# Linear attention with both heads of a pair in one 128-row product, and the low parts of keys written in place

## The chip, the cores and the metric

The kernel runs on one core of a Trainium2 chip. The metric is the time of the whole program on the device, in microseconds. TensorE is called PE here, its weight loads PEld, VectorE DVE, ScalarE ACT, GpSimd POOL and SyncE SP; SP issues nearly all DMAs.

## The reference

Two transformer blocks over 512 tokens of 1024 features. The first mixes gated linear attention (4 heads of 64), sliding-window attention (8 query heads, 2 key heads of 64), a pooling branch and gates, then a feed-forward layer. The second has forgetting attention (16 heads of 64), a feed-forward layer, latent attention and a feed-forward layer. What the change touches:

```python
# linear attention, per head; b is the running sum of log gates in a chunk
attn = einsum('bhid,bhjd,bhijd->bhij', q, k, exp(b_i - b_j))     # j <= i
o    = einsum('bhij,bhjv->bhiv', attn, v) + einsum('bhid,bhdv->bhiv', q * exp(b), S)
# window attention and forgetting attention, per head
s = einsum('qd,kd->qk', q, k) * 64 ** -0.5      # + mask, or + gate bias; then softmax, then @ v
```

## The kernel before

Activations lie with features on partitions and tokens along the free axis. A projection is made for 128 outputs at a time: eight 128-row blocks of inputs, each block with three f32r products of 512 columns (high by high, high by low, low by high; `mm3`, line 347). Weights stream through SP into `raw`, ACT makes the high part, DVE the low part (`lo`, line 277).

Each attention is a Python generator. Every matmul that is recorded adds to a counter (`clock`, line 338), and `tick` resumes a generator once the counter passes its due time. The table `LAG` holds the due times. So the order of PE's instructions is fixed by these numbers; a scheduler orders those of the other engines. At most four generators are active. All PSUM banks (8) are shared by everything, and so are 39 SBUF slots of 4 KB a partition.

**Linear attention** (`gla`, line 678) builds for each head the 512 masked weights in `A`: one diagonal product and seven levels with distance s = 64, 32, ... 1. For each level `mixed` multiplies the keys on one side and the queries on the other by decay factors (DVE d, ACT exponential, POOL and DVE `mix`), and `masked` makes four products of 128 by 128 for each of four heads. A head has 64 features, and so these products have 64 rows; they are f32. A masked copy on DVE (line 703) brings each bank into `A`. Later come the states `S` between blocks of 128 tokens, and the outputs `o`, where full-row products by `A` and 64-row products by `S` take turns. The result is wanted only when gate a begins, long after the pooling projections `pu`, the gate projections `gr` and the gates c and b. The PE instructions of the mixer follow in the order gv, sv, sk, sq, pu, gr, poolw, gate c, gate b, gate a.

**Scores** of the window attention (`swa`) and of the forgetting attention (`fox`) have queries `Q` with the high part in 64 rows and the low part in the other 64, so that one product by `K` (high part of the key in both halves) makes two terms; a second by `L` (low part) adds the rest. `stack_k` (line 432) makes KH on ACT and KL on DVE and copies each half four times by DMA. The forgetting attention does so for eight pairs of heads, the window attention once.

Of the kernel before, what the change touches and what calls it, by code (L numbers as in the profile page):

```python
# [24 lines left out]
LEVELS = (64, 32, 16, 8, 4, 2, 1)  # L25
# [130 lines left out]
def tfk_kept(e):  # L156
# [12 lines left out]
    "last": 2.8, "last_rsqrt": 3.7,  # L169
    "decay": 8.0, "level": 1.85, "mask": 1.22, "state": 6.5, "kt": 1.44, "U": 1.95, "osq": 4.41, "gnorm": 6.82, "gbc": 0.8,  # L170
    "fox_gap": 4.38, "mla_gap": 4.48, "swa_gap": 3.75, "swa": 4.0, "swa_soft": 14.0, "swa_pt": 8.0, "fox": 6.04, "fox_soft": 22.08, "fox_last": 0.8, "fox_pt": 4.44,
# [24 lines left out]
class Net:  # L196
    def __init__(self, ctx, tc, xin, wall, par, cst, msk, nar, out, dbg=None):
        self.tc, self.nc = tc, tc.nc
        nc = self.nc
# [5 lines left out]
        self.psum = ctx.enter_context(tc.tile_pool(name="psum", bufs=8, space=bass.MemoryType.PSUM))  # L205
        self.nslot, self.nt2 = 39, 9
        self.x = [self.slot([P, 2, T], F32, "x") for _ in range(4)]
# [5 lines left out]
        self.ones = self.cpool.tile([P, P], F32, name="ones")  # L213
        nc.gpsimd.memset(self.ones, 1.0)
        self.ident = self.c("ident", 128)
        self.unit_at = 0
# [215 lines left out]
    def stack_k(self, k):  # L432

        nc = self.nc
        out = K, L = [self.slot([P, 2, T], F32R, n) for n in ("K", "L")]
        parts = [self.t2(dt=F32R, name=n) for n in ("KH", "KL")]
        nc.scalar.copy(out=parts[0], in_=k)
        nc.vector.tensor_tensor(out=parts[1], in0=k, in1=parts[0].bitcast(F32), op=ALU.subtract)
        for a, b in zip(out, parts):
            for j in range(2):  # L440
                for r in range(2):
                    nc.sync.dma_start(out=a[64 * r:64 * r + 64, j].bitcast(F32), in_=b[64 * j:64 * j + 64].bitcast(F32))
        return K, L

    def mm_stacked(self, out, Q, K, L, j, qs, ks):

        self.mm(out, Q[:, j, qs], K[:, j, ks], True, False)
        self.mm(out, Q[:, j, qs], L[:, j, ks], False, True)

# [126 lines left out]
    def mixer(self, nxt):  # L576
        nc, v = self.nc, self.nc.vector
# [4 lines left out]
        glow = self.narrow("glow")  # L582
# [4 lines left out]
        pl = self.proj_narrow(glow, self.xs)  # L587
# [3 lines left out]
        rsb, rst = self.rs.get()  # L591
        glow = self.t2([16, T], F32, "glow")
        v.tensor_tensor(out=glow, in0=self.add_narrow(pl, 32, 16), in1=rsb[0:16], op=ALU.mult)
        b = self.slot([P, 2, T], F32, "b")
# [6 lines left out]
        for f in range(2):  # L601
            ps = first[f]
# [75 lines left out]
    def gla(self, glow, b, kT, qT, vtok, fut):  # L678
        nc, v = self.nc, self.nc.vector
        reset = self.c("reset", 512)  # L680
        for f in range(2):
            pz = self.ps("z")
            self.mm(pz, self.c("gup", 256)[0:16, f * P:(f + 1) * P], glow, True, True)
            la = self.t2(name="la")
            self.log_sigmoid(pz, self.p("b_gate", f), (P, T), la)
            v.tensor_tensor_scan(out=b[:, f], data0=reset, data1=la, initial=0.0, op0=ALU.mult, op1=ALU.add)
            yield LAG["decay"]
        A = [self.slot([P, 2, T], F32, "A") for _ in range(2)]
        Ah = [A[h // 2][:, h % 2] for h in range(4)]
        for a in A:  # L690
            nc.gpsimd.memset(a, 0.0)
        while not self.qk_ready:
            yield 1.0
        yield 1.0

        def masked(li, mixq, mixk):
            for h in range(4):
                f, r = h // 2, slice(64 * (h % 2), 64 * (h % 2) + 64)
                ps = self.ps("lev")
                for m in range(4):  # L700
                    c = slice(m * P, (m + 1) * P)
                    self.mm(ps[:, c], mixk[r, f, c], mixq[r, f, c], True, True)
                v.copy_predicated(
                    out=Ah[h].rearrange("p (m i) -> p m i", m=4), mask=self.msk[:, li].unsqueeze(1).to_broadcast([P, 4, P]),
                    data=ps.rearrange("p (m i) -> p m i", m=4))
                yield LAG["mask"]

        def mixed(s):
# [5 lines left out]
            d = self.slot([P, 2, T], F32, "d")  # L714
            mix = self.slot([P, 2, T], F32, "mix")
            bv, dv, mv = view(b), view(d), view(mix)
# [4 lines left out]
            nc.gpsimd.tensor_tensor(out=mv[:, :, 0:s], in0=dv[:, :, 0:s], in1=view(kT)[:, :, 0:s], op=ALU.mult)  # L721
            v.tensor_tensor(out=mv[:, :, s:], in0=dv[:, :, s:], in1=view(qT)[:, :, s:], op=ALU.mult)
            return mix

        nxt = mixed(LEVELS[0])
        yield from masked(len(LEVELS), qT, kT)
        for li, s in enumerate(LEVELS):
            mix = nxt
            if li + 1 < len(LEVELS):
                nxt = mixed(LEVELS[li + 1])  # L730
            yield LAG["level"]
            yield from masked(li, mix, mix)

# [35 lines left out]
        for h in range(4):  # L769
            f, r = h // 2, slice(64 * (h % 2), 64 * (h % 2) + 64)  # L770
# [32 lines left out]
    def swa(self, t, g, q, k, V, of, fut):  # L803
# [13 lines left out]
        for n in range(4):  # L817
            lo, out = where(n)
            keys = slice(max(n - 1, 0) * P, (n + 1) * P)
            self.mm_stacked(out, q, *k, g, slice(n * P, (n + 1) * P), keys)  # L820
        for n in range(4):
# [216 lines left out]
    def fox(self, nxt):  # L1038
# [40 lines left out]
        def head(h, q, k, bias, of, fut):  # L1079
# [6 lines left out]
            m0 = self.tiny([P, 4], F32, "m0")  # L1086
            for n in range(4):
                w = (n + 1) * P
                self.mm_stacked(sc[n], q, *k, j, slice(n * P, w), slice(0, w))
            for n in range(4):  # L1090
# [297 lines left out]
```

## Time and profile before

| | |
|---|---|
| Time before, median of 3 runs | 2256.32 us (2255.63 to 2258.09) |
| The profiled execution | 2253.59 us |
| Its span | 2251.7 us |
| Mean granted clock of PE | 0.991 |
| PE busy | 2196.6 us (98%) |
| DVE busy | 1415.0 us (63%) |
| ACT busy | 1020.5 us (45%) |

The mixer's linear and window attention lie between about 62 and 207 us, the forgetting attention between about 850 and 1110. PE's busy time is modelled from its records and also covers time in which its pipe only empties; so a stretch is read by the starts of its instructions. A matmul in f32 leaves two records, one in f32r leaves one.

### The profile page before, as it was taken

To read this page: it belongs to the slowest core of one execution; us is meant where nothing else is said; L and a number is where in the kernel's file an instruction comes from. 1 tells how busy PE (TensorE), PEld (TensorE's weight loads), DVE (VectorE), ACT (ScalarE), POOL (GpSimd) and SP (SyncE) were. 2 spreads that over 40 slices of the span, in tenths; PEclk is the share of its full clock that TensorE was granted. 3 is DMA by queue.
4 is the path that set the end of the run, shared out by engine and by line. 5 is a ranking of instruction groups with operands and counts; after the bars stand their busy time and mean duration, and the time that the engine had idled before them with its cause. 6 is when DMAs were issued, how large, how long until landed. Compare 5 with 4: busy or idle time off the path is not lost.

```text
span 2251.7 us, 27823 instructions
## 1 busy us (share of the span) xinstructions
PE 2196.6 (98%) x10664; PEld 1837.5 (82%) x10664; DVE 1415.0 (63%) x2349; ACT 1020.5 (45%) x1672; POOL 279.2 (12%) x231
## 2 busy tenths in 40 slices
PE   8999999999999998988999999999999999999998
PEld 6778888898888897867888888887888888888887
DVE  7798445578776247657667775357656557777624
ACT  4354333444444235556544443235756665444322
POOL 4122000040000003445200000102100101000000
PEclk9999999999999999999999999999999999999998
DMA  4201333332333343634233333332122213333232
GB/s 161 76 29 57 96 101 94 113 94 69 101 94 98 99 131 116 167 105 112 76 94 100 97 94 101 96 108 75 57 66 66 75 57 94 94 100 97 94 101 96
DMA packets 64838, 211.04 MB, mean 94 GB/s; under 512 B 7728, under 2 KB 10160, under 8 KB 64704
## 3 DMA queue, kind: packets, MB, share of 16 engines
q1 hardware_dynamic: 64272, 208.46, 30.9%
q8 instruction: 84, 1.38, 0.3%
q10 hardware_dynamic: 432, 0.79, 0.1%
q14 instruction: 50, 0.41, 0.1%
HBM read 197.65 MB, written 2.13 MB: 89 GB/s over the span
## 4 chain that ended last, share of the span: by engine, by line
PE 85%; DVE 8%; ACT 3%; DMA 2%; issue 2%; SPq 1%; POOL 0%; DVEq 0%; ACTq 0%; POOLq 0%
PE up L339 31%; PE down L339 15%; PE mout L339 4%; PE uq L339 3%; PE sc L339 3%; PE gate_a L339 2%; PE gate_b L339 2%; PE gate_c L339 2%; PE fout L339 2%; PE wout L339 2%; DVE lo L277 2%; PE lev L339 1%; DVE xs L420 1%; PE mpo L339 1%; PE dq L339 1%
## 5 line engine op out<-in xcount | busy, mean ns | idle before, releaser
L277 DVE TENSOR_TENSOR lo<-raw,hi 128x1024 fp32r<-128x1024 f32 (+1 forms) x348 | 438.4, 1260 | 327.2 <-ACT hi L276 322.8
L339 PE MATMUL up<-xs,hi 128*128 128x512 f32 x2016 | 621.7, 390 | 0.0
L276 ACT CAST hi<-raw 128x1024 fp32r<-128x1024 f32 (+1 forms) x348 | 365.3, 1050 | 563.6 <-PE down L339 171.8
L339 PEld LDWEIGHTS up<-xs,hi 128*128 128x128 f32 x2016 | 378.2, 188 | 79.5 <-issue 1.0
L339 PE MATMUL up<-xs,lo 128*128 128x512 f32 x1008 | 392.2, 389 | 0.0
L339 PE MATMUL down<-hl,hi 128*128 128x512 f32 (+1 forms) x1188 | 332.9, 366 | 0.0
L339 PEld LDWEIGHTS down<-hl,hi 128*128 128x128 f32 x1188 | 214.8, 189 | 36.4
L339 PEld LDWEIGHTS up<-xs,lo 128*128 128x128 f32 x1008 | 189.2, 188 | 39.1
L339 PE MATMUL down<-hl,lo 128*128 128x512 f32 (+1 forms) x594 | 217.1, 365 | 0.0
L503 POOL TENSOR_TENSOR acc<-acc,sq 128x256 f32<-128x256 f32 (+1 forms) x48 | 56.1, 1169 | 765.2 <-ACT sq L500 763.5
L980 DVE TENSOR_TENSOR u<-up,rsb 128x512 f32<-128x512 f32 x132 | 90.2, 686 | 80.9 <-PE up L339 76.7
L982 ACT ACTIVATE c<-u,par 128x512 f32<-128x512 f32 x132 | 107.0, 814 | 60.0 <-DVE u L980 59.8
L339 PEld LDWEIGHTS down<-hl,lo 128*128 128x128 f32 x594 | 112.0, 189 | 17.8
L983 DVE SCALAR_TENSOR_TENSOR c<-u,par,c 128x511 f32<-128x511 f32 x132 | 98.4, 747 | 23.8 <-ACT c L982 23.8
L919 POOL TENSOR_TENSOR x<-x,yo 128x256 f32<-128x256 f32 x32 | 28.9, 939 | 608.0 <-DVE yo L918 608.0
L984 DVE SCALAR_TENSOR_TENSOR c<-u,par,c 128x510 f32<-128x510 f32 x132 | 98.9, 749 | 4.0
L339 PE MATMUL uq<-hl,hi 128*128 128x512 f32 x288 | 89.5, 391 | 1.4 <-POOL hl L454 1.4
L453 ACT CAST hl<-c 128x512 fp32r<-128x512 f32 x66 | 40.8, 617 | 104.6 <-DVE c L991 104.6
L339 PE MATMUL mout<-hl,hi 128*128 128x512 f32 x256 | 79.8, 393 | 0.0
L989 ACT ACTIVATE c<-c 128x512 f32<-128x512 f32 x66 | 41.6, 630 | 70.1 <-DVE c L984 70.0
L420 DVE SCALAR_TENSOR_TENSOR xs<-x,par,xs 128x512 fp32r<-128x512 f32 (+1 forms) x64 | 62.0, 1007 | 7.9 <-ACT xs L419 7.9
L339 PEld LDWEIGHTS uq<-hl,hi 128*128 128x128 f32 x288 | 53.9, 188 | 13.3 <-POOL hl L454 1.8
(392 smaller groups left out, 3953.1 us busy)
## 6 DMA issues: line engine op xcount, KB each, us to landing
raw<-in_wall_dram SPq DMA_DIRECT2D x359, 512.0 KB, 3.6
K<-KH SPq DMA_DIRECT2D x36, 128.0 KB, 2.3
L<-KL SPq DMA_DIRECT2D x36, 128.0 KB, 2.3
bias<-cumd SPq DMA_DIRECT2D x16, 256.0 KB, 4.5
out_dram<-x SPq DMA_DIRECT2D x8, 256.0 KB, 2.4
x<-in_x_dram SPq DMA_DIRECT2D x7, 256.0 KB, 5.3
raw<-in_wall_dram SPq DMA_DIRECT2D x2, 256.0 KB, 3.9
early<-in_cst_dram SPq DMA_DIRECT2D x1, 512.0 KB, 6.5
```

Source lines behind the costliest of these rows:

```text
L276: nc.scalar.copy(out=hi[:, c], in_=raw[:, c])
L277: nc.vector.tensor_tensor(out=lo[:, c], in0=raw[:, c], in1=hi[:, c].bitcast(F32), op=ALU.subtract)
L339: self.nc.tensor.matmul(out, lhsT=a, rhs=b, start=start, stop=stop)
L420: nc.vector.scalar_tensor_tensor(out=lo, in0=src, scalar=scale, in1=hi.bitcast(F32), op0=ALU.mult, op1=ALU.subtract)
L453: nc.scalar.copy(out=hi, in_=src)
L503: (eng or self.nc.vector).tensor_tensor(out=acc[:, cols], in0=acc[:, cols], in1=sq[:, cols], op=ALU.add)
L919: nc.gpsimd.tensor_tensor(out=x, in0=x, in1=yt, op=ALU.add)
L980: v.tensor_tensor(out=u, in0=ps, in1=rsb, op=ALU.mult)
L982: nc.scalar.activation(out=c, in_=u, func=AF.Identity, scale=self.p(conv, 88 + t), bias=self.p(conv, 132 + t))
L983: v.scalar_tensor_tensor(out=c[:, 1:], in0=u[:, 0:T - 1], scalar=self.p(conv, 44 + t), in1=c[:, 1:], op0=ALU.mult, op1=ALU.add)
L984: v.scalar_tensor_tensor(out=c[:, 2:], in0=u[:, 0:T - 2], scalar=self.p(conv, t), in1=c[:, 2:], op0=ALU.mult, op1=ALU.add)
L989: nc.scalar.activation(out=g, in_=g, func=func)
```

## The change

Linear attention: two query tiles `pads` hold the two heads of a pair side by side, each in its own 64 rows with zeros in the other 64, and the keys lie in `kmix`, whose query positions stay zero. One product of all 128 rows then makes the weights of both heads. Of each level only the 64 query positions of a block are sent through, so that a bank holds two heads; the masked copies take 256 columns each instead of 512. The outputs by `S` and the small gate product `z` also get 128 rows with zeros. Keys: the low part is written by DVE into one of two fixed tiles `lows`, whose other halves are zero, and is no longer copied by DMA; the term low by low falls away. Seven due times of the linear attention grow, and the slots fall from 39 to 37.

```diff
 LAG = {
...
-    "decay": 8.0, "level": 1.85, "mask": 1.22, "state": 6.5, "kt": 1.44, "U": 1.95, "osq": 4.41, "gnorm": 6.82, "gbc": 0.8,
+    "decay": 8.0, "level": 4.0, "mask": 1.8, "state": 8.0, "kt": 2.5, "U": 3.0, "osq": 4.41, "gnorm": 12.0, "gbc": 1.6,
...
-        self.nslot, self.nt2 = 39, 9
+        self.nslot, self.nt2 = 37, 9
...
+        self.lows = [self.cpool.tile([P, 2, T], F32R, name=f"lows{i}") for i in range(2)]
...
     def stack_k(self, k):
...
-        out = K, L = [self.slot([P, 2, T], F32R, n) for n in ("K", "L")]
-        parts = [self.t2(dt=F32R, name=n) for n in ("KH", "KL")]
-        nc.scalar.copy(out=parts[0], in_=k)
-        nc.vector.tensor_tensor(out=parts[1], in0=k, in1=parts[0].bitcast(F32), op=ALU.subtract)
-        for a, b in zip(out, parts):
-            for j in range(2):
-                for r in range(2):
-                    nc.sync.dma_start(out=a[64 * r:64 * r + 64, j].bitcast(F32), in_=b[64 * j:64 * j + 64].bitcast(F32))
+        K = self.slot([P, 2, T], F32R, "K")
+        L = self.lows[0]
+        self.lows.reverse()
+        H = self.t2(dt=F32R, name="KH")
+        nc.scalar.copy(out=H, in_=k)
+        for j in range(2):
+            r = slice(64 * j, 64 * j + 64)
+            nc.vector.tensor_tensor(out=L[r, j], in0=k[r], in1=H[r].bitcast(F32), op=ALU.subtract)
+        for j in range(2):
+            for r in range(2):
+                nc.sync.dma_start(out=K[64 * r:64 * r + 64, j].bitcast(F32), in_=H[64 * j:64 * j + 64].bitcast(F32))
         return K, L
...
-        glow = self.t2([16, T], F32, "glow")
-        v.tensor_tensor(out=glow, in0=self.add_narrow(pl, 32, 16), in1=rsb[0:16], op=ALU.mult)
+        glow = self.t2([P, T], F32, "glow")
+        nc.gpsimd.memset(glow, 0.0)
+        for a in self.lows:
+            for j in range(2):
+                nc.gpsimd.memset(a[64 - 64 * j:128 - 64 * j, j].bitcast(F32), 0.0)
+        v.tensor_tensor(out=glow[0:16], in0=self.add_narrow(pl, 32, 16), in1=rsb[0:16], op=ALU.mult)
...
-            self.mm(pz, self.c("gup", 256)[0:16, f * P:(f + 1) * P], glow, True, True)
+            self.mm(pz, self.c("gup", 256)[:, f * P:(f + 1) * P], glow, True, True)
...
+        pads = [self.slot([P, 2, T], F32, "pad") for _ in range(2)]
+        rows = [slice(64 * j, 64 * j + 64) for j in range(2)]
+        for a in pads:
+            for j in range(2):
+                nc.gpsimd.memset(a[rows[1 - j], j], 0.0)
+        kmix = [self.slot([P, 2, T], F32, "kmix") for _ in range(2)]
+        for a in kmix:
+            nc.gpsimd.memset(a, 0.0)
...
+        def mixed(li):
...
+            d, kx, qx = self.slot([P, 2, T], F32, "d"), kmix[li % 2], pads[li % 2]
...
+            nc.gpsimd.tensor_tensor(out=view(kx)[:, :, 0:s], in0=dv[:, :, 0:s], in1=view(kT)[:, :, 0:s], op=ALU.mult)
+            for j, r in enumerate(rows):
+                v.tensor_tensor(out=qx[r, j].rearrange("p (n c) -> p n c", c=s), in0=dv[r, :, s:], in1=view(qT)[r, :, s:], op=ALU.mult)
+
+        def level(li):
...
+            for f in range(2):
+                ps = self.ps("lev")
+                for m in range(4):
+                    q = qx[:, :, f * 256 + m * 64:f * 256 + m * 64 + 64]
+                    self.mm(ps[:, m * P:(m + 1) * P], kx[:, f, m * P:(m + 1) * P], q, True, True)
+                out = ps.rearrange("p (m j n c) -> p m j n c", m=4, j=2, c=s)
+                for j in range(2):
+                    v.copy_predicated(out=queries(Ah[2 * f + j]), mask=mask, data=out[:, :, j])
+                yield LAG["mask"]
+
+        def diagonal():
...
+            for f in range(2):
+                for j, r in enumerate(rows):
+                    nc.scalar.copy(out=pads[f][r, j], in_=qT[r, f])
+            for f in range(2):
+                for m0 in (0, 2):
+                    ps = self.ps("lev")
+                    for m in (m0, m0 + 1):
+                        c = slice(m * P, (m + 1) * P)
+                        self.mm(ps[:, (m - m0) * 256:(m - m0) * 256 + 256], kT[:, f, c], pads[f][:, :, c], True, True)
+                    out = ps.rearrange("p (m j i) -> p m j i", m=2, j=2)
+                    for j in range(2):
+                        v.copy_predicated(
+                            out=Ah[2 * f + j][:, m0 * P:m0 * P + 256].rearrange("p (m i) -> p m i", m=2), mask=mask, data=out[:, :, j])
+                    yield LAG["mask"]
...
-        v.tensor_tensor(out=qe, in0=qe, in1=qT, op=ALU.mult)
+        for f in range(2):
+            for j, r in enumerate(rows):
+                v.tensor_tensor(out=pads[f][r, j], in0=qe[r, f], in1=qT[r, f], op=ALU.mult)
...
-                    self.mm(po[:, c], S[r, f, m - 1], qe[r, f, c], False, True)
+                    self.mm(po[:, c], S[:, f, m - 1], pads[f][:, j, c], False, True)
```

How instructions move, at three places. On PE, where the diagonal products begin (`lev` are the products, `gv` and `sv` projections), before:

```order
L339 MATMUL lev<-qT,kT 128x128 x4
L339 MATMUL gv_345<-hi,xs 128x512
L339 MATMUL gv_345<-lo,xs 128x512
L339 MATMUL gv_345<-hi,xs 128x512
L339 MATMUL lev<-qT,kT 128x128 x4
L339 MATMUL gv_346<-hi,xs 128x512
L339 MATMUL gv_346<-lo,xs 128x512
L339 MATMUL gv_346<-hi,xs 128x512
L339 MATMUL lev<-qT,kT 128x128 x4
```

and now:

```order
L340 MATMUL lev<-pad,kT 128x256 x2
L340 MATMUL sv<-xs,hi 128x512 x2
L340 MATMUL sv<-xs,lo 128x512
L340 MATMUL sv<-xs,hi 128x512 x2
L340 MATMUL sv<-xs,lo 128x512
L340 MATMUL lev<-pad,kT 128x256 x2
```

There are as many banks, but now a bank holds two products of 256 columns, all full rows, and six projection products lie between banks. In the levels behind it there are two banks of four products in place of four banks of four. On DVE, just ahead of the first states `S` (`sc<-sc,den` scales the window attention's weights, 128 rows of one head per four), before:

```order
L834 RECIPROCAL den<-den 128x4
L277 TENSOR_TENSOR lo<-raw,hi 128x1024
L837 TENSOR_SCALAR sc<-sc,den 128x128
L837 TENSOR_SCALAR sc<-sc,den 128x256 x3
L762 COPY S<-U 64x128 x2
L764 SCALAR_TENSOR_TENSOR S<-S,dec,U 64x128 x3
```

and now:

```order
L877 TENSOR_TENSOR den<-den,es 128x4
L878 RECIPROCAL den<-den 128x4
L881 TENSOR_SCALAR sc<-sc,den 128x128
L881 TENSOR_SCALAR sc<-sc,den 128x256 x3
L914 TENSOR_TENSOR swo<-swo,half 64x512
L458 TENSOR_TENSOR hl<-pd,hl 128x512
L806 COPY S<-U 64x128 x2
L458 TENSOR_TENSOR hl<-swo,hl 128x512
L808 SCALAR_TENSOR_TENSOR S<-S,dec,U 64x128 x4
```

Before, the fourth head's weights stand ahead of the first `S`; now it is the eighth's. On SP, in the forgetting attention around one pair's keys (`raw` are weights, `bias` rows of gates), before:

```order
L442 DMA K<-KH 64x512 x4
L442 DMA L<-KL 64x512 x4
L1075 DMA bias<-cumd 128x512 x2
L275 DMA raw<-in_wall_dram 128x1024 x2
L442 DMA K<-KH 64x512 x4
L442 DMA L<-KL 64x512 x4
L1075 DMA bias<-cumd 128x512 x2
```

and now:

```order
L446 DMA K<-KH 64x512 x4
L1119 DMA bias<-cumd 128x512 x2
L276 DMA raw<-in_wall_dram 128x1024 x2
L446 DMA K<-KH 64x512 x4
L1119 DMA bias<-cumd 128x512 x2
```

The copies of the low part are gone, and what stood behind them moves up. On PE everything behind gate c's first two banks stands in the same order as before.

## Rows read from the trace of the kernel before

**Rows 1.** The page, part 1: busy time, share of the span and instructions of each engine.

```profile
PE 2196.6 (98%) x10664; PEld 1837.5 (82%) x10664; DVE 1415.0 (63%) x2349; ACT 1020.5 (45%) x1672; POOL 279.2 (12%) x231
```

**Rows 2.** Windows of core 0: stretch, its length, busy of each engine, PEclk, DMA share, GB/s.

```profile
62.00:207.00 145.00, 142.56 (x810) 112.85 (x809) 124.14 (x270) 61.93 (x141) 31.63 (x24) 1.00 0.17 48
207.00:297.00 90.00, 90.00 (x398) 74.51 (x397) 50.72 (x64) 31.50 (x41) 9.38 (x12) 1.00 0.31 94
850.00:1110.00 260.00, 234.37 (x1157) 194.78 (x1158) 173.46 (x457) 153.13 (x329) 103.09 (x85) 0.95 0.41 116
```

**Rows 3.** Timeline of PE: start, us, engine, line, op, tiles, shape; projections and products.

```profile
60.59 0.62 PE L339 MATMUL gv<-hi,xs 128*128 128x512 f32 x2
61.27 0.62 PE L339 MATMUL gv<-hi,xs 128*128 128x512 f32 x2
62.27 1.16 PE L339 MATMUL lev<-qT,kT 64*128 64x128 f32 x8
63.36 0.50 PE L339 MATMUL gv<-hi,xs 128*128 128x512 f32 x1
64.25 1.16 PE L339 MATMUL lev<-qT,kT 64*128 64x128 f32 x8
...
296.56 0.62 PE L339 MATMUL gate_b<-xs,hi 128*128 128x512 f32 x2
```

**Rows 4.** Timeline of PE: a 128-row f32 product before f32r products.

```profile
39.03 1.02 PE L339 MATMUL bc<-diag,ones 128*128 128x512 f32 x2
40.12 0.40 PE L339 MATMUL gv<-lo,xs 128*128 128x512 f32 x1
```

**Rows 5.** Timeline of PE: output products of one head.

```profile
167.30 0.69 PE L339 MATMUL o<-A,vt 128*128 128x128 f32 x4
167.93 0.48 PE L339 MATMUL o<-qe,S 64*128 64x128 f32 x2
168.34 0.49 PE L339 MATMUL o<-A,vt 128*128 128x128 f32 x2
```

**Rows 6.** DVE instructions by line and form, 62 to 207: x count | busy, mean ns | idle.

```profile
L703 DVE COPY_PREDICATED A<-msk,lev 128x512 f32<-128x512 int32 x32 | 23.5, 737 | 10.0 <-PE lev L339 9.8
L454 DVE TENSOR_TENSOR swp<-swt,swp 128x512 fp32r<-128x512 f32 x8 | 5.4, 679 | 0.0
L454 DVE TENSOR_TENSOR swp<-swt,swp 128x384 fp32r<-128x384 f32 x8 | 4.4, 547 | 0.0
```

**Rows 7.** The tile mix: DVE's products, duration min/median/max in ns.

```profile
L722 DVE TENSOR_TENSOR mix<-d,qT x7: 679/891/1755, 68.1 to 124.7; 128x512 f32<-128x512 f32 x7
```

**Rows 8.** Waits of PE, 820 to 1110: total us, times, longest us.

```profile
PE sc L339 <- DMA L<-KL: 14.1, 7, 5.3
PE sc L339 <- DMA K<-KH: 2.9, 2, 1.7
PE fpo L339 <- DVE ptl L454: 1.4, 4, 0.5
PE t L344 <- DVE mx L1096: 1.3, 1, 1.3
```

**Rows 9.** Windows of 5 us in the forgetting attention.

```profile
975.00:980.00 5.00, 1.28 (x5) 1.31 (x6) 0.96 (x4) 1.97 (x4) 2.46 (x2) 0.69 1.00 263
980.00:985.00 5.00, 4.91 (x18) 3.78 (x17) 2.82 (x16) 1.56 (x7) 2.51 (x2) 0.62 0.02 7
1005.00:1010.00 5.00, 4.71 (x20) 3.83 (x20) 3.24 (x16) 0.54 (x3) 1.29 (x1) 0.73 0.78 221
1050.00:1055.00 5.00, 3.42 (x11) 2.97 (x12) 3.92 (x12) 2.08 (x4) 0.00 (x0) 0.70 0.77 193
```

**Rows 10.** Timeline of SP's queue and DVE around one pair's scores.

```profile
969.01 3.40 SPq L442 DMA_DIRECT2D K<-KH  x4
971.33 0.68 DVE L438 TENSOR_TENSOR KL<-fk,KH 128x512 fp32r<-128x512 f32 x1
973.22 2.39 SPq L442 DMA_DIRECT2D L<-KL  x4
```

More of the change, by code (lines that the diff above doesn't have):

```diff
@@ L434, in stack_k, with mm_stacked @@
         nc = self.nc
-        out = K, L = [self.slot([P, 2, T], F32R, n) for n in ("K", "L")]
-        parts = [self.t2(dt=F32R, name=n) for n in ("KH", "KL")]
-        nc.scalar.copy(out=parts[0], in_=k)
-        nc.vector.tensor_tensor(out=parts[1], in0=k, in1=parts[0].bitcast(F32), op=ALU.subtract)
-        for a, b in zip(out, parts):
-            for j in range(2):
-                for r in range(2):
-                    nc.sync.dma_start(out=a[64 * r:64 * r + 64, j].bitcast(F32), in_=b[64 * j:64 * j + 64].bitcast(F32))
+        K = self.slot([P, 2, T], F32R, "K")
[9 more added lines that the diff above has]
+                nc.sync.dma_start(out=K[64 * r:64 * r + 64, j].bitcast(F32), in_=H[64 * j:64 * j + 64].bitcast(F32))
         return K, L
-    def mm_stacked(self, out, Q, K, L, j, qs, ks):
-        self.mm(out, Q[:, j, qs], K[:, j, ks], True, False)
-        self.mm(out, Q[:, j, qs], L[:, j, ks], False, True)
+    def mm_stacked(self, outs, Q, K, L, j):
+        for out, qs, ks in outs:
+            self.mm(out, Q[:, j, qs], K[:, j, ks], True, False)
+            self.mm(out, Q[:, j, qs], L[:, j, ks], False, True)
     def split(self, src, out=None, eng=None):
@@ L691, in gla @@
             nc.gpsimd.memset(a, 0.0)
+        pads = [self.slot([P, 2, T], F32, "pad") for _ in range(2)]
[6 more added lines that the diff above has]
+            nc.gpsimd.memset(a, 0.0)
         while not self.qk_ready:
             yield 1.0
[L694 to L708, printed above, removed]
+        yield 3.0
+        def mixed(li):
+            s = LEVELS[li]
             nb = 1024 // (2 * s)
@@ L712, in view @@
                 return t.rearrange("p f (n c) -> p (f n) c", c=2 * s)
-            d = self.slot([P, 2, T], F32, "d")
-            mix = self.slot([P, 2, T], F32, "mix")
-            bv, dv, mv = view(b), view(d), view(mix)
+            d, kx, qx = self.slot([P, 2, T], F32, "d"), kmix[li % 2], pads[li % 2]
+            bv, dv = view(b), view(d)
             ref = bv[:, :, s - 1:s].to_broadcast([P, nb, s])
@@ L720, in mixed @@
             nc.scalar.activation(out=d, in_=d, func=AF.Exp, scale=1.0 / 16.0)
[L721 to L728, printed above, removed]
+            nc.gpsimd.tensor_tensor(out=view(kx)[:, :, 0:s], in0=dv[:, :, 0:s], in1=view(kT)[:, :, 0:s], op=ALU.mult)
@@ new lines, in mixed, with queries @@
+            for j, r in enumerate(rows):
+                v.tensor_tensor(out=qx[r, j].rearrange("p (n c) -> p n c", c=s), in0=dv[r, :, s:], in1=view(qT)[r, :, s:], op=ALU.mult)
+        def level(li):
+            s = LEVELS[li]
+            kx, qx = kmix[li % 2], pads[li % 2]
+            def queries(t):
+                return t.rearrange("p (m n c) -> p m n c", m=4, c=2 * s)[:, :, :, s:]
+            mask = self.msk[:, li].rearrange("p (n c) -> p n c", c=2 * s)[:, :, s:].unsqueeze(1).to_broadcast([P, 4, 64 // s, s])
+            for f in range(2):
[7 more added lines that the diff above has]
+                yield LAG["mask"]
@@ new lines, in diagonal @@
+        def diagonal():
+            mask = self.msk[:, len(LEVELS)].unsqueeze(1).to_broadcast([P, 2, P])
+            for f in range(2):
[12 more added lines that the diff above has]
+                    yield LAG["mask"]
@@ L729, in gla @@
+        yield from diagonal()
+        mixed(0)
+        for li in range(len(LEVELS)):
             if li + 1 < len(LEVELS):
-                nxt = mixed(LEVELS[li + 1])
+                mixed(li + 1)
             yield LAG["level"]
-            yield from masked(li, mix, mix)
+            yield from level(li)
         qe = self.slot([P, 2, T], F32, "qe")
@@ L769, in gla @@
         for h in range(4):
-            f, r = h // 2, slice(64 * (h % 2), 64 * (h % 2) + 64)
+            f, j = divmod(h, 2)
             po = self.ps("o")
@@ L819, in swa @@
             keys = slice(max(n - 1, 0) * P, (n + 1) * P)
-            self.mm_stacked(out, q, *k, g, slice(n * P, (n + 1) * P), keys)
+            self.mm_stacked([(out, slice(n * P, (n + 1) * P), keys)], q, *k, g)
         for n in range(4):
@@ L1086, in head @@
             m0 = self.tiny([P, 4], F32, "m0")
-            for n in range(4):
-                w = (n + 1) * P
-                self.mm_stacked(sc[n], q, *k, j, slice(n * P, w), slice(0, w))
+            self.mm_stacked([(sc[n], slice(n * P, (n + 1) * P), slice(0, (n + 1) * P)) for n in range(4)], q, *k, j)
             for n in range(4):
```

## The prediction

> **What bounds the kernel now.** First the page: PE is busy for 98% of the span, DVE for 63% [rows 1]. So the kernel lasts as long as PE's list, and the question at each place is what stretches that list and whether another engine can follow when it shrinks. Then the windows: from 62 to 207 us, where linear and window attention run between projections, PE is without work for 145 - 142.6 = 2.4 us only, while DVE is busy for 124.1 of 145, and behind it, to 297, for 50.7 of 90 [rows 2]. In the forgetting attention PE is busy for 234.4 of 260 at a mean clock of 0.95 [rows 2]. PE's timeline says what stretches the first stretch (the 64-row products), its waits and the 5 us windows what stretches the second.
>
> **Linear attention, on PE.** Three projection products take 0.68 from start to start (the first two rows of [rows 3]). A bank of four 64-row products takes 1.09, and the three projection products behind it 0.89 until the next bank starts [rows 3]. An f32 product of 512 columns and all 128 rows, followed by one f32r product of 0.227, takes 1.09 together [rows 4]: so 0.86 for 512 columns, 0.215 for 128, and nothing extra between f32 and f32r. Four products are then worth 0.86, and a bank of 64-row products pays 1.09 - 0.86 + 0.89 - 0.68 = 0.44 for going to 64 rows and back. The outputs show the same: two full-row products worth 0.43 take 0.63 ahead of a 64-row one, and that one, worth 0.215, takes 0.41 [rows 5], 0.2 per turn.
>
> What goes: 32 such banks by 0.44 = 14.1; 56 of the levels' 112 products by 0.215 = 12.0 (the diagonal keeps its columns); in the outputs 4 heads by 6 turns by 0.2 = 4.8; the two gate products about 0.6 (16 rows, counted at 0.3 each as a bank's turns less what they share, an estimate). Sum 31.5, and 34 if the 2.4 of idle time went too. Gate b, which starts at 296.6 [rows 3], would start at 263.
>
> The Trainium skill, TensorEngine Tiling (Array Packing), Key Properties, says that changing the tiling mode drains the engine, as the 0.2 above, but also that tiles work independently and in parallel. By that second sentence two heads' 64-row products could overlap, padding would gain no product time, and the sum on PE would be 12 less. Here the four products of a bank lie in the same 64 rows and follow one another at 0.215, so I keep the 12.
>
> **Linear attention, on DVE.** Its work does not shrink. Masked copies: 32 by 0.737 = 23.6 before [rows 6]; now 36 of half the columns. Between 384 and 512 columns an instruction grows by 0.679 - 0.547 = 0.132 [rows 6], so 256 columns less save 0.264: 0.47 each, 17.0 in sum, between 13.3 (half of 0.737 each) and 26.5 (nothing saved). Queries by decay: 7 at a median of 0.89 [rows 7] become 14, since each covers 64 partitions at the same 512 columns: 14 by 0.8 = 11.2, between 9.5 (0.679 each) and 24.6 (1.755 each). The output queries: one product of 1024 columns, about 1.3, becomes four of 0.68. The key's low part: one of 0.68 becomes two. In all -6.6 + 4.9 + 1.4 + 0.7 = 0.4: nothing. The four new copies on ACT (busy 61.9 of 145 [rows 2]) and the zero fills on POOL (31.6 of 145) are hidden by those engines' idle time; without that cover the fills, some ten instructions below 1 us, would move the first bank by under 10.
>
> So PE's list loses 31.5 of 145 and DVE's none, and DVE becomes the late one. How late is seen where the outputs begin. The order shows that the first states now stand behind the scaling of all eight window heads, not of four; so PE's first output product waits for most of DVE's list. Of the 124.1 that DVE does to 207 [rows 2], what now stands behind those states is the other states, four output copies, the norm with its four diagonals and four products, and a little of the window attention: about 20 instructions near 0.68 and some 20 small ones. I take 16, so 108 stand ahead. PE's diagonal now starts behind the nine projection products that lay between banks, at 62.3 + 9 by 0.227 - 0.6 = 64. DVE begins 1 later, needs 108, and waits a little: before it was idle for 21 of 145, half of that for PE's banks [rows 2, 6]; a late engine waits less, and I take 8, between 0 and 21. The outputs then begin at 64 + 1 + 108 + 8 = 181. What PE has from there to gate b: 381 projection products by 0.227 = 86.5, 28 output products by 0.215 = 6, ten broadcasts and small groups by at most 0.86 = 8.4: 101. Gate b at 282, 14.6 earlier than before. PE's own list would have been there at 263 - 101 = 162; it stands still for 19 us in several pieces. What that costs in clock is seen in the forgetting attention below; I take 2.5 for it and for later small waits. **Linear attention gains 12**, between 1 (DVE idle for 21) and 24 (DVE idle for 0, cheapest copies).
>
> **Forgetting attention.** PE waits 14.1 us in 7 pieces for the copied low part [rows 8]. Behind long waits the clock falls: in the windows shown it is 0.62 to 0.73, and busy time by what is missing gives 1.28 x 0.31 + 4.91 x 0.38 + 4.71 x 0.27 + 3.42 x 0.30 = 4.6 us [rows 9]. Both hang on one chain: K's copies are issued at 969.0 and take the queue 3.4, KL is ready at 972.0, its copies follow at 973.2 and take 2.4 to issue [rows 10], and PE waited up to 5.3 for them [rows 8]. Now the low part is in place two half-instructions behind KH; from 971.3 that is 972.7, before the old copies were even issued. The four transfers also leave the queue ahead of `bias` and the weights. Late next is K itself: PE waited for it twice, 2.9 in sum [rows 8], and K left about 2.5 before the low part. DVE pays 0.68 more per pair, busy 173 of 260 [rows 2]. And the softmax loses the time that PE's waits gave it: for it PE waits 1.3 and 1.4 now [rows 8]. I take 5 for all that comes back, four more waits like the 1.3; the bounds are 0 and 14 (each removed wait comes back shorter by 2.5 at most and some clock stays lost). **Gain 14.1 + 4.6 - 5 = 14**, between 5 and 19.
>
> Nothing else changes on PE. The two slots less are matched by one L per pair less in the forgetting attention; in the mixer two query tiles come on top, which I cover by the range.
>
> **Sum.** 12 + 14 = 26 from the profiled execution's 2253.6 us (span 2251.7 and 1.9 around it) gives 2227.6. The median shown is 2.7 above that execution; on it, 2230.
>
> **Rivals.**
> - *PE's list decides alone.* DVE would follow because its queue holds much that PE doesn't need at once. For it: DVE has 39 us free from 207 to 297 [rows 2]. Against it: the states stand behind all eight heads in DVE's one queue. Gains of 24 and 18, 2256 - 42 = 2214.
> - *K takes L's place.* For it: K waits exist, up to 1.7, and K needs its own four issues and a landing [rows 8, 10]. Against it: in the longest wait K was there. Then the forgetting attention gains 5, and the whole 17: 2239.
> - *Both are absorbed.* DVE idles as much as before (gain 1) and half the second gain returns as softmax waits (3): 2252, and with one more us lost in the mixer it is within 0.2%.
> - *Slower: the new DVE forms cost their worst row.* One mechanism at both places: products of two SBUF inputs, split into half-partition pieces, held up while POOL works beside them. One such instruction took 1.755 against 0.679 at the least [rows 7]. If all 14 took that (+13.4), the 36 copies 0.74 (+9.5) and the 4 output queries 1.755 (+4.3), the outputs begin 27 later and the mixer loses 15 in place of gaining 12; 16 half low parts at 1.755 lay 17 on DVE in the forgetting attention, which takes all of its 14. 2256 + 15 = 2271. It decides against the gain from about 1.3 us per new instruction. For it only the one row; against it the median of 0.89 in the same company.
>
> The Trainium skill, SBUF — State Buffer, SBUF: two separate sides, says that a GpSimd instruction and a VectorE one with two SBUF inputs hold the shared port exclusively and the loser blocks. By that rule doubling the products does not double the blocking, since POOL's instructions stay seven, which is between my 0.8 and the worst row.
>
> **Chances.** Forecast (gains of 18 to 34) 0.58, PE alone 0.12, K in L's place 0.20, absorbed 0.06, slower 0.04. A difference of 0.2%, 4.5 us, is what a measurement here can tell from none. Faster takes the first three and a third of the fourth: 0.92; same 0.04; slower 0.04. The likeliest case's own range is 2222 to 2238; eight in ten lie between 2211, PE alone with a little more, and 2245, K in L's place with a poorer mixer.
>
> **What would show it.** Right: banks of products at 0.86 or 0.43 per 256 columns and projections at 0.68 behind them; PE waiting some 15 to 20 us between the window attention's transposes and the first output for DVE; gate b at 278 to 286; no wait on a copied low part, waits on K below 6 us, clock near 0.98 in the forgetting attention. Wrong: gate b before 275 or behind 292, turns of 0.2 around full-row products, masked copies over 0.6, DVE's products over 1.2, or waits on K of 10 us.

## The result and the profile after

The changed kernel takes 2224.49 us (median of 4 runs, 2222.04 to 2228.24), the kernel before 2255.98 beside it (2252.63 to 2258.09): ratio 0.9863, 95% interval 0.9845 to 0.9882. Faster by 1.4%; the forecast was 2230, with a range of 2211 to 2245. The profiled execution after took 2225.05 (span 2223.3; before 2251.7), and the numbers of this section compare these two executions. Gate b starts 5.4 us earlier (291.2), the last product of `fout` ends its stretch 27.9 earlier, and the later stages are as long as they were. So linear attention gave 5.4 where 12 was forecast, and the forgetting attention 22.3 where 14 was forecast, more than its upper bound of 19.

The page of after, part 1 [rows 1]: PE is still what the kernel lasts for.

```profile
PE 2165.1 (97%) x10536; PEld 1822.0 (82%) x10536; DVE 1423.7 (64%) x2372; ACT 1022.2 (46%) x1676; POOL 282.1 (13%) x242
```

The windows of after that answer to [rows 2], and the mixer from 62 to gate b (before: 234.6 long, PE busy 232.2).

```profile
62.00:207.00 145.00, 126.45 (x711) 108.81 (x710) 129.91 (x284) 67.95 (x148) 36.41 (x35) 0.95 0.17 51
207.00:297.00 90.00, 89.30 (x393) 72.37 (x392) 47.27 (x70) 26.51 (x34) 0.00 (x0) 1.00 0.29 88
850.00:1110.00 260.00, 252.41 (x1279) 211.72 (x1278) 196.10 (x477) 162.02 (x341) 110.09 (x85) 0.99 0.36 108
62.00:291.20 229.20, 209.95 (x1076) 176.35 (x1075) 175.06 (x350) 93.40 (x181) 36.41 (x35) 0.97 0.22 65
```

PE's work shrank, and PE did not use all of it: in the first window it is busy for 16 us less, idle for 18.6 us, and DVE is busy for 129.9 of 145.

PE's timeline of after, a bank of level products between projections [rows 3] and the outputs of a head [rows 5].

```profile
79.16 0.62 PE L340 MATMUL sk<-xs,hi 128*128 128x512 f32 x2
79.86 1.05 PE L340 MATMUL lev<-pad,kmix 128*128 128x128 f32 x8
80.66 0.70 PE L340 MATMUL sk<-xs,hi 128*128 128x512 f32 x2
81.44 0.62 PE L340 MATMUL sk<-xs,hi 128*128 128x512 f32 x2
...
188.35 0.61 PE L340 MATMUL o<-A,vt 128*128 128x128 f32 x4
188.79 0.39 PE L340 MATMUL o<-pad,S 128*128 128x128 f32 x2
189.02 0.39 PE L340 MATMUL o<-A,vt 128*128 128x128 f32 x2
```

A bank takes 0.80 (79.86 to 80.66) and the three projection products behind it 0.78: 1.58 where 1.98 was paid before and 1.54 was forecast. Among the outputs nothing is left of the turns: 0.44 for two products, 0.23 for one.

DVE's groups of after, 62 to 207, as [rows 6], and then the row of the new query products with min, median and max in ns, as [rows 7].

```profile
L730 DVE TENSOR_TENSOR pad<-d,qT 64x512 f32<-64x512 f32 x14 | 14.6, 1040 | 0.1
L747 DVE COPY_PREDICATED A<-msk,lev 128x256 f32<-128x256 int32 x28 | 12.8, 520 | 2.3 <-PE lev L340 2.3
L764 DVE COPY_PREDICATED A<-msk,lev 128x256 f32<-128x256 int32 x8 | 2.9, 435 | 0.0
```

```profile
L730 DVE TENSOR_TENSOR pad<-d,qT x14: 674/706/1692, 71.0 to 140.8; 64x512 f32<-64x512 f32 x14
```

The masked copies cost 15.7 in all (17.0 forecast), the query products 14.6 (11.2 forecast). Neither is even. Of the levels' 28 copies twenty took 0.41 to 0.45, but the eight of the last two levels (s = 2 and 1, where the columns lie in runs of two and one) 0.72 to 0.80, as long as 512 columns took before. Of the query products eight took 0.67 to 0.72 and six 1.10 to 1.69. The six are those that began well inside a product of POOL (`kmix`, or the window attention's `Q`), as the pair here:

```profile
88.98 1.29 POOL L728 TENSOR_TENSOR kmix<-d,kT 128x512 f32<-128x512 f32 x1 [15.77 <-ACT d L727]
89.31 3.20 DVE L730 TENSOR_TENSOR pad<-d,qT 64x512 f32<-64x512 f32 x2
90.44 3.22 POOL L430 TENSOR_TENSOR Q<-sq__700,Q 64x512 fp32r<-64x512 f32 x2 [0.18 <-ACT Q L429]
```

PE's waits in the mixer of after, 62 to 291: total us, times, longest us. Before there were three, 2.3 in sum.

```profile
PE swt L345 <- DVE sc L881: 6.4, 5, 3.0
PE U L340 <- ACT kt L797: 4.5, 1, 4.5
PE swas L340 <- POOL Q L430: 2.5, 1, 2.5
PE svt L345 <- issue: 2.3, 1, 2.3
PE swas L340 <- DVE swp L458: 1.4, 1, 1.4
PE swo L340 <- DVE swo L914: 1.2, 1, 1.2
```

Of the window attention `swas` are the scores, `swt` the transposes of its weights, `svt` those of its values and `swo` its outputs; `U` are the products for the states, made with the transposed keys `kt`. The largest single wait, 4.5 on ACT, is DVE's at one remove. ACT's timeline there:

```profile
170.39 0.30 ACT L873 ACTIVATE es<-nm,par 128x4 f32<-128x4 f32 x1 [5.13 <-DVE nm L871]
...
174.93 0.48 ACT L797 COPY kt<-kdt 128x384 f32<-128x384 f32 x1
```

The transposes `kdt` were done at 166.5; ACT has the copy `kt` queued behind the exponentials of two window heads, and for those it stood still for 5.13 until DVE had their maximum.

The windows of 5 us between 62 and gate b in which the clock was not full (columns as [rows 2]; before there was none).

```profile
122.00:127.00 5.00, 3.01 (x16) 3.02 (x16) 4.78 (x10) 1.23 (x2) 0.51 (x1) 0.66 0.00 0
147.00:152.00 5.00, 2.71 (x12) 1.95 (x13) 5.00 (x12) 1.85 (x3) 2.58 (x4) 0.87 0.37 105
152.00:157.00 5.00, 5.00 (x26) 4.45 (x26) 5.00 (x12) 0.62 (x2) 0.00 (x0) 0.79 0.37 105
172.00:177.00 5.00, 1.54 (x4) 1.27 (x5) 4.70 (x17) 4.38 (x15) 0.83 (x2) 0.76 0.00 0
177.00:182.00 5.00, 5.00 (x16) 3.92 (x15) 3.43 (x10) 0.89 (x2) 0.00 (x0) 0.56 0.00 0
```

Each stands at or right behind a wait of PE. Busy time by what is missing at the clock: 1.0 + 0.4 + 1.0 + 0.4 + 2.2 = 5.0 us.

The forgetting attention from the first `fk` to the last `fout`: the window of before, and then that of after.

```profile
911.80:1128.10 216.30, 196.12 (x968) 163.04 (x968) 140.02 (x391) 130.67 (x295) 95.15 (x70) 0.96 0.42 115
```

```profile
906.20:1100.20 194.00, 188.52 (x968) 158.78 (x967) 149.29 (x399) 130.07 (x295) 96.75 (x70) 0.99 0.36 107
```

PE's waits of after in it [rows 8]:

```profile
PE sc L340 <- DMA K<-KH: 3.0, 2, 1.7
PE fpo L340 <- DVE ptl L458: 2.1, 4, 0.9
```

Two more are of 0.2 each. Of the 22.3 us, 14.7 are idle time of PE (20.2 to 5.5) and 7.6 are busy time of the same 968 products, at a mean clock of 0.99 in place of 0.96.

### The profile page after: what moved, and what is told of

Read it like the earlier page. It is cut to its first block, busy times and chain, and to the rows that moved or that the text cites. A ratio compares the mean times of both kernels' runs of the same rounds, so it can differ in the third digit from the quotient of the medians.

```text
span 2223.3 us, 27520 instructions
## 1 busy us (share of the span) xinstructions
PE 2165.1 (97%) x10536; PEld 1822.0 (82%) x10536; DVE 1423.7 (64%) x2372; ACT 1022.2 (46%) x1676; POOL 282.1 (13%) x242
## 4 chain that ended last, share of the span: by engine, by line
PE 84%; DVE 9%; ACT 3%; issue 2%; DMA 1%; POOL 0%; SPq 0%; DVEq 0%; ACTq 0%; POOLq 0%
PE up L340 32%; PE down L340 15%; PE mout L340 4%; PE uq L340 3%; PE sc L340 2%; PE gate_a L340 2%; PE gate_b L340 2%; PE gate_c L340 2%; PE wout L340 2%; PE fout L340 2%; DVE lo L278 2%; DVE xs L421 1%; PE mpo L340 1%; PE dq L340 1%; PE fq L340 1%
```

## The experiments

All times are medians of 4 to 6 runs; the kernel before, on the same chip each time, took 2254.7 to 2256.2. "After" is 2224.5 and its profile.

**1. The keys alone**: `stack_k` and its fixed tiles as after, all else as before.

> Only the part on the keys: the low part goes straight into a zero-padded fixed tile, linear attention and its distances are as before. Theory: the forgetting attention's gain comes from this part alone, 14.7 us of waits and 7.6 us of slow clock, and needs nothing of the other part: 22 us faster than before, about 2233; the stretch from the first fk to the last fout 194 us (216.3 before), gate b at 296 to 297 as before. Rival: part of the 22.3 comes from the later stages falling differently against the mixer's end, or the window attention also gains from its low part: then 5 us or more lie outside that stretch. My prediction's size of this part (14) would give 2242.

Measured: 2230.7, ratio 0.9888 (0.9873 to 0.9903). From first `fk` to last `fout`:

```profile
911.90:1105.80 193.90, 188.43 (x967) 158.77 (x966) 147.81 (x399) 130.19 (x295) 96.99 (x70) 0.99 0.36 107
```

The 194 of after, without the other part. Gate b is at 297.7, 1.1 late. The theory holds; my 14 was too small. The rival asked for 5 us outside that stretch; by the medians 2.6 of 25.0 lie there, by the profiled spans 0.2 of 22.6.

**2. Linear attention alone**: as after, with the old `stack_k` and 39 slots.

> Only the part on linear attention, with the longer distances; the low part of the keys is copied as before. Theory: gate b at 291 and 5 us faster than before, about 2250, with the waits on L in the forgetting attention back at 14 us. Rival: the DVE work for the low parts holds up the mixer (two half instructions in place of one, and zero fills on POOL), so without it gate b is at 288 or earlier and the kernel 8 us or more faster than before. My prediction's size of this part (12) would give 2244.

Measured: 2247.5, ratio 0.9962 (0.9948 to 0.9975); 8.2 below before, 6.4 in the profiled spans. Gate b at 288.7, the waits on L back (12.4, and 6.1 on K). That lies between the theory and the rival, nearer to the rival. In the mixer the fixed low part with its zero fills costs a little: gate b is at 291.2 with it and 288.7 without, and PE's wait on `Q`, which POOL writes, is 2.5 with it and 0.7 without. The sum of both parts, 25 + 8, is about the whole 31.5.

**3. The distances of before** in the changed kernel.

```
-"level": 4.0, "mask": 1.8, "state": 8.0, "kt": 2.5, "U": 3.0, "gnorm": 12.0, "gbc": 1.6
+"level": 1.85, "mask": 1.22, "state": 6.5, "kt": 1.44, "U": 1.95, "gnorm": 6.82, "gbc": 0.8
```

> The changed kernel with the distances of before (level 1.85, mask 1.22, state 6.5, kt 1.44, U 1.95, gnorm 6.82, gbc 0.8). Theory: DVE's list decides when the outputs begin, and the distances only set where in PE's list the waiting instructions stand: shorter ones put PE's products ahead of DVE's readiness, so PE stands longer at the levels, 2 to 8 us slower than the changed kernel, about 2229. Rival 1: the longer distances are what put the states behind all eight window heads and cost the mixer its gain; then the old ones give 5 us or more back, 2219 or below. Rival 2: no effect, within 2 us, since DVE's queue is the same in sum.

Measured: 2223.8, ratio 0.9860 (0.9843 to 0.9877): no effect that can be measured, the second rival. The rows of the first and last starts of the outputs and of gate b's first kind of product:

```profile
L340 PE MATMUL o<-A,vt x32: 275/275/356, 144.7 to 163.5; 128*128 128x128 f32 x32
...
L340 PE MATMUL gate_b<-xs,hi x128: 389/389/390, 288.9 to 351.0; 128*128 128x512 f32 x128
```

The outputs start at 144.7 in place of 188.3, and gate b is only 2.3 earlier. So the start of the outputs, by which I had reckoned, does not lead to gate b: PE's idle time just falls elsewhere (17.9 us in all, 19.2 after).

**4. The window attention's scaling on ACT.**

```
-v.tensor_scalar(out=sc[:, n, lo:], in0=sc[:, n, lo:], scalar1=den[:, n:n + 1], ...)
+nc.scalar.activation(out=sc[:, n, lo:], in_=sc[:, n, lo:], func=AF.Copy, scale=den[:, n:n + 1])
```

> The changed kernel with the scaling of the window attention's probabilities (32 instructions of 0.41 to 0.49 us) on ACT in place of DVE. Theory: DVE's list decides the mixer between 62 and 188 us; 15 us less on DVE bring the first output 10 to 14 us earlier, PE's waits on sc (6.4 us) and most of the slow clock (5 us) go, gate b at 279 to 283, the kernel at 2213 to 2217. Rival: PE's waits come from distances and from chains of single steps, not from DVE's list; then ACT's longer chain per head (its scalings cost some 0.45 each as well) moves nothing, gate b at 290 to 293, 2223 to 2227.

Measured: 2218.0, ratio 0.9837 (0.9820 to 0.9855), gate b at 284.9. The waits on `sc` are gone, the other waits stay (`kt` 4.5, `Q` 2.5, `svt` 2.3, `swp` 1.7). Between the two: the scalings that left DVE kept it busy for 13.6 us there (10.3 for the 24 of 256 columns and 3.3 for the 8 of 128), and 6.3 came back.

**5. The masked copies twice, and 6. none.** In the first each of the levels' copies is made twice, in the second they are left out.

```
-for j in range(2):
+for j in (0, 1, 0, 1):
     v.copy_predicated(out=queries(Ah[2 * f + j]), mask=mask, data=out[:, :, j])
```

> The changed kernel, with each of the levels' 28 masked copies done twice: 28 by 0.52 = 14.6 us more on DVE, nothing else changed. Theory: DVE's list decides the mixer, it is without work for less than 10 us between 62 and 188; gate b comes 11 to 15 us later, 302 to 306, the kernel at 2235 to 2240. Rival: single chains (scores, scaling, transposes; states, kt, U) decide and DVE has slack between them; then less than 5 us later, under 2230.

> The changed kernel without the levels' 28 masked copies (their products are made, but do not reach the attention matrix): 14.6 us less on DVE, PE's list the same. Theory: DVE's list decides, and PE has 19 us of waits and 5 us of slow clock to give back, so gate b comes 9 to 14 us earlier, 277 to 282, the kernel at 2210 to 2216. Rival: single chains decide, as the scaling on ACT may be read (15 us off DVE gave 6.5 us): then 5 us or less, 2219 or more.

Measured: twice 2236.9, ratio 0.9918 (0.9905 to 0.9932); none 2218.7, ratio 0.9834 (0.9821 to 0.9848). The mixer from 62 to gate b, first twice, then none:

```profile
62.00:301.60 239.60, 217.18 (x1075) 181.73 (x1074) 187.17 (x378) 93.83 (x181) 36.77 (x35) 0.94 0.20 62
```

```profile
62.00:284.40 222.40, 209.14 (x1074) 176.22 (x1073) 163.53 (x322) 93.49 (x181) 40.06 (x35) 0.97 0.22 67
```

12.1 us more on DVE (187.2 against 175.1) move gate b by 10.4: more work on DVE is paid nearly in full. But only 3.2 of the 10.4 are idle time of PE (22.4 against 19.2); 7.2 are longer busy time of the same products, at a mean clock of 0.94 in place of 0.97. 11.5 us less give 6.8, of which 6.0 are idle time: work taken away comes back by little more than half, since other chains (`U` on `kt` 3.8, `swas` on `swp` 4.7) stand close behind. The theory holds upwards only; the rival's 5 is nearer downwards.

**7. Longer distances for window attention and states.** `swa` is the head start of a head's scores, `swa_soft` the distance from the softmax to the transposes, `swa_pt` from there to the output; 1.5 is that of the values.

```
-"swa": 4.0, "swa_soft": 14.0, "swa_pt": 8.0, "kt": 2.5
+"swa": 6.5, "swa_soft": 22.0, "swa_pt": 10.0, "kt": 8.0
-self.spawn(self.swa_values(sv, V), 1.5)
+self.spawn(self.swa_values(sv, V), 4.5)
```

> The changed kernel with longer distances for the window attention and the states: head start 6.5 (4.0), softmax to transposes 22 (14), transposes to output 10 (8), kt 8 (2.5), values 4.5 (1.5). PE has projections up to gate b that need none of this, and DVE is without work for some 39 us of the last 84 before gate b. Theory: DVE's list decides only as long as PE's waiting instructions stand close behind it; farther behind, PE's 19 us of waits shrink to 5 to 10 and the slow clock to 2, gate b at 276 to 283, the kernel at 2209 to 2217. Rival: DVE's load decides in any order, PE's waits only move behind, gate b at 288 to 293, 2221 to 2227, as with the old, shorter distances.

Measured: 2218.1, ratio 0.9832 (0.9819 to 0.9846), gate b at 282.7. DVE has as much work as after (177.7), and only two waits are left:

```profile
PE kdt L345 <- DVE kd L784: 8.4, 1, 8.4
PE swo L340 <- DVE pd L933: 4.3, 1, 4.3
```

The theory's direction, but less than it asked for: the time is 1 us behind its range, PE is idle for 13.1 us and not 5 to 10, and by the 5 us windows the clock takes 6.0 and not 2. Gate b lies at the slow end of its range; the rival, 288 or later, is out. Both waits stand before an instruction whose distance was still short.

**8. Both**: as 7, with 20 for `state` and 14 for `swa_pt`, and the scaling of 4.

> The longer distances once more, with the two waits that the last run still showed moved too (states 20 in place of 8, transposes to output 14 in place of 10), and the window attention's scaling on ACT in place of DVE. Theory: PE's waits come from how close the waiting instructions stand behind DVE's queue and from how long that queue is, and both can be eased; of the 13 us of waits and 6 of slow clock that the last run had left up to gate b, about 5 and 2 remain: gate b at 269 to 275, the kernel at 2203 to 2211. Rival: both edits ease the same waits and new ones come up (ACT's queue, tiles held longer), so that the two gains of 6.5 us don't add: 2214 to 2219.

Measured: 2206.2 (2203.0 to 2207.7), ratio 0.9778 (0.9765 to 0.9791): 18 us faster than after and the fastest version here. Runs 4 and 7 gave 6.5 and 6.4, 13 together. This run also lengthened two distances further; whether the other 5 us are theirs was not run. From 62 to gate b:

```profile
62.00:270.00 208.00, 204.07 (x1075) 173.07 (x1074) 167.00 (x318) 104.63 (x213) 43.88 (x35) 0.99 0.24 71
```

PE is idle for 3.9 us and loses 1.5 at the clock. Without those gate b would be at 264.6; my reckoning for PE's list alone was 263.

**9. The outputs' state products on 64 rows** again, in the changed kernel.

```
-self.mm(po[:, c], S[:, f, m - 1], pads[f][:, j, c], False, True)
+self.mm(po[:, c], S[rows[j], f, m - 1], pads[f][rows[j], j, c], False, True)
```

> The changed kernel, with linear attention's 24 output products that read the states on the head's 64 rows alone again, as before (the other rows are zeros). DVE's list is the same. Theory: each turn to 64 rows and back costs 0.2 us of PE, and from the first output on PE has no wait to hide it: 24 products with 24 returns, taken as 24 by 0.2 = 4.8 us, gate b at 296, the kernel at 2229. Rival 1: a turn is hidden or products in different rows overlap; then within 1 us of the changed kernel. Rival 2: the first rows of before count one turn in and one out, 48 by 0.2 = 9.6 us, 2234.

Measured: 2232.1, ratio 0.9896 (0.9883 to 0.9910); gate b 8.4 later. PE's timeline, one head:

```profile
190.62 0.61 PE L340 MATMUL o<-A,vt 128*128 128x128 f32 x4
191.16 0.48 PE L340 MATMUL o<-pad,S 64*128 64x128 f32 x2
191.58 0.49 PE L340 MATMUL o<-A,vt 128*128 128x128 f32 x2
...
193.24 0.72 PE L340 MATMUL gr<-xs,hi 128*128 128x512 f32 x2
```

A head takes 2.62 here and 1.48 after (188.35 to 189.83): 1.14 for 6 turns, 0.19 each, 4.6 for four heads, as the theory had it (4.8). The waits are those of after; the rest of the 8.4 is clock, 8.8 us lost against 5.0 by the same windows. The Trainium skill, TensorEngine Tiling (Array Packing), Key Properties, says that a change of the tiling mode drains the engine; the trace fits that, at 0.19 a turn.

**10. The copies of the low part still issued**, into a tile that nobody reads: a rotating one (a), or a fixed one with 36 slots (b); and 36 slots alone (c).

```
+D = self.slot([P, 2, T], F32R, "D")        # (b): D = self.D
+for j in range(2):
+    r = slice(64 * j, 64 * j + 64)
+    for i in range(2):
+        nc.sync.dma_start(out=D[64 * i:64 * i + 64, j].bitcast(F32), in_=L[r, j].bitcast(F32))
```

> The changed kernel, with four copies of the low part still issued per key pair at their old place (36 in all, into a tile that nobody reads). Theory: what the forgetting attention gained is the wait for the copies' landing and the slow clock behind those waits, not the transfers or their place in SP's queue; so the time stays at 2223 to 2228, no wait over 2 us comes back, and the stretch from the first fk to the last fout is 194 to 198 us. Rival: the queue was the cost, since bias, weights and K stand behind these copies; then K's waits rise above 8 us and half of the 22 us is given back, 2234 or more.

> As the run with the copies kept, but these go into one fixed tile and not into a rotating one, and one rotating slot is taken away for it (36 in place of 37). The earlier run was 13 us slower than the changed kernel without a longer wait on K; it could be the transfers (four more issues of 0.6 per pair in SP's one queue and 2.3 to land, with bias and weights behind them) or the rotating slot that they held, which SP's queue had to wait for. Theory queue: still 10 to 14 us slower than the changed kernel less what 36 slots cost by themselves, 2234 to 2240. Theory slot: within 3 us of the run with 36 slots alone.

> The changed kernel with 36 rotating slots in place of 37. Theory queue: the slots are not scarce, within 3 us of the changed kernel, 2222 to 2228. Theory slot: one slot less holds up the forgetting attention or the mixer by 5 us or more, 2230 or above.

Measured: (a) 2237.4, ratio 0.9924 (0.9911 to 0.9936); (b) 2228.5 (2222.3 to 2233.6), ratio 0.9879 (0.9863 to 0.9896); (c) 2225.1, ratio 0.9864 (0.9849 to 0.9879). My theory failed for (a): half of the 22 us went although nobody waits for the copies, and not by the wait on K that the rival named. PE's waits of (a), 906 to 1112, and the stretch:

```profile
PE fpo L340 <- DVE ptl L463: 3.8, 7, 1.2
PE sc L340 <- DVE pts L463: 2.4, 1, 2.4
PE fpo L340 <- ACT pth L462: 2.2, 2, 1.7
PE t L345 <- DVE mx L1143: 1.6, 1, 1.6
PE sc L340 <- DMA K<-KH: 1.3, 1, 1.3
```

```profile
906.00:1112.10 206.10, 194.13 (x967) 160.94 (x966) 148.08 (x399) 130.45 (x295) 95.63 (x70) 0.98 0.43 121
```

It is the softmax that comes late. So the 22.3 us have two parts. Copies that nobody waits for leave the stretch at 206.1, 10.2 below before; without them it is 194.0, another 12.1. One slot less costs nothing by itself (c).

What of the copies costs those 12 us is not settled. By the medians 8.9 of the 13 us go with a fixed tile, the intervals of (a) and (b) do not touch, and the transfers are left with 3.4 ((b) against (c), whose intervals overlap); that would lay most of it on the rotating tile. But the executions of (b) spread over 11 us, and in the profiled one, the slowest, most of the loss is still there. The stretch in (b), and then in (c):

```profile
906.30:1108.50 202.20, 193.05 (x967) 161.37 (x966) 149.95 (x399) 130.16 (x295) 96.30 (x70) 0.97 0.44 123
```

```profile
907.10:1099.60 192.50, 187.00 (x968) 157.47 (x967) 147.34 (x399) 130.13 (x295) 97.23 (x70) 1.00 0.37 107
```

By which tile or transfer the softmax is delayed is not shown either.

## Why the prediction was right and wrong

The time was right by luck: its two halves were wrong by 6.6 and 8.3 us in opposite directions. Gate b, at 291.2, lies between the signs set for right (278 to 286) and for wrong (behind 292).

**Linear attention** (12 forecast, 5.4 measured), from 62 to gate b:

| us | forecast | measured |
|---|---|---|
| PE's work at full clock | -31.5 | -27.2 (232.2 to 209.95 - 5.0) |
| PE idle | +16.6 (2.4 to 19) | +16.8 (2.4 to 19.2) |
| slow clock | +2.5 | +5.0 |

- *0.44 per bank, 0.2 per turn in the outputs, 0.215 per product*: right. 1.58 for a bank and what follows against 1.54; 0.19 per turn in run 9. The list's term was too large by some 4 all the same. The clock's share is a sum over coarse windows, and by the runs with the same list and other waits the list is 202 to 206 long, a gain of 26 to 31.
- *DVE becomes the late one*: right in kind and size (19.2 us of waits, some three quarters of it on DVE or through it), and run 5 shows it by adding work. The terms of the chain came near: DVE was busy for 114.6 us between 64.8 and the outputs (108 forecast) and idle for 8.9 (8 forecast), and from the outputs to gate b it took 102.9 (101 forecast). So they started at 188 and not 181. As a floor the chain was wrong: "PE's first output product waits for most of DVE's list" is the step that failed. Run 3 moves the outputs to 145 for 2.3 us at gate b. PE waits wherever its instructions stand too close behind DVE's, and with other distances the same DVE work costs 13 us of waits (run 7), and with a shorter list and still longer distances 4 (run 8).
- *2.5 for the clock*: half of what it was; five windows lose 5.0. By my own figures of the other stage (4.6 us of clock for 14.1 of waits) 19 us would have cost 6.
- *Query products at 0.8*: 1.04 in the mean; the median is 0.71, and the six that met POOL took 1.10 to 1.69. My argument that POOL's instructions stay seven left out that its `Q` products meet them too. That adds 3.4 to DVE, which at run 5's price is 2.9 at gate b.
- *Masked copies at 0.47*: right in the sum (15.7 against 17.0), but as a mix of 0.41 to 0.45 and, for eight, 0.72 to 0.80, which is over the 0.6 named as a sign of being wrong.
- *The rival that PE's list alone decides* needed gate b at 263. It was not so in this kernel, though DVE had 54 us free up to gate b (busy for 175.1 of 229.2). With longer distances, and the scalings off DVE, run 8 comes to 270.

**Forgetting attention** (14 forecast, 22.3 measured).

- *14.1 for the waits on L*: right; they are gone. Run 10 (a) shows that this alone was not all: the copies cost 12 us even where nobody waits for them, and the prediction had no term for that.
- *5 that come back*: the step that failed on this side. Waits on K and the softmax are 5.5 after and were 5.8 before; K did not take L's place (3.0 after 2.9). In run 10 (a) such waits do come, with the rotating tile; my reasons for them (less slack for the softmax, DVE's 0.68 more per pair) did not bring them.
- *4.6 for the clock*: too small. I had summed four windows; the whole stretch lost 7.6 us of busy time. Windows of 5 us, all of them this time, put 7.0 us at the clock before and 1.5 after, so 5.5 of the 7.6; the rest I can't attribute.
- *Low part at 0.68 per half*: the 16 have a median of 0.69, hidden as forecast.

The slower case (DVE's worst form everywhere) did not come: of the query products two reached 1.7, of the sixteen low parts one 1.8, and of the masked copies eight came to the 0.74 or so that it took for all.

Two sums of the prediction do not come out. The lower bound of linear attention leaves out the clock: 14.6 - 13 - 2.5 is -1, not 1. And half of the second gain is 7, not 3, so the rival in which both are absorbed gives 2248, not 2252.

## What to carry to other kernels

When an engine's list shrinks and the next one becomes late, what is lost depends on how close the waiting instructions stand behind it: moving them farther back in a strict order can be worth as much as taking work away (6.4 and 6.5 us here), and the two can be had together (18 us, with distances longer still). A wait of the matrix engine costs its length and then often slow clock: a quarter to a half of it in the two stages here (5.0 for 19.2 us, 7.6 for 14.7), but a single wait of 1.9 us cost no clock in the kernel before and 1.7 us in run 1. So sum the clock over the whole stretch, and over more than one execution. Before a stage's first late result is taken for its bound, check that anything needs that result then.

## What the runs showed of the hardware

- The clock also fell where PE's records show no wait. In run 9, behind the single-column sums and the 64-row outputs of the last head (start, us):

```profile
210.72 0.95 PE L340 MATMUL gsum<-ones,osq 128*128 128x1 f32 x8
211.53 0.69 PE L340 MATMUL o<-A,vt 128*128 128x128 f32 x4
...
216.40 0.63 PE L340 MATMUL gr<-xs,lo 128*128 128x512 f32 x1
...
218.43 0.40 PE L340 MATMUL gr<-xs,lo 128*128 128x512 f32 x1
```

  From 214 to 218 the projection products take 0.63 in place of 0.40; the granted clock is 0.50 from 215 to 217, which is 1.2 GHz and not 2.4. In after, the same place with 128-row outputs keeps the full clock (1.00 from 205 to 215). Run 1 shows the fall a second time: behind the single-column sums and 64-row outputs from 166.1 to 169.6 the granted clock is 0.50 from 170 to 173, with PE busy throughout. The kernel before has the same instructions there and kept the full clock; what more it takes is open.
- The spans of the four runs of after follow the granted clock: they are 2220.3, 2222.1, 2223.3 and 2226.4 at mean clocks of 0.993, 0.992, 0.991 and 0.989. Differences of 3 us between kernels here are within that.
- Elementwise products of 64 partitions by 512 columns last as long on DVE as those of 128 partitions (0.69 at the median for the low parts, 0.68 before).
